# A ring of weight slots: taking a kept slot's entry out of the queue of pools

## The chip, the core and the metric

The kernel runs on one core of a Trainium2 chip. The metric is device time in microseconds (us), taken as the median of several runs. The five engines named below are TensorE (PE; PEld is its weight load), VectorE (DVE), ScalarE (ACT), GpSimd (POOL) and SyncE (SP), whose queue issues nearly all transfers. "DMA" is the core's 16 DMA engines taken together.

## What is computed

One block of a streaming encoder for 256 rows of width 2048: a projection and two kinds of attention, an output projection, and then a mixture of 32 small expert networks, of which each row uses two. Everything the change touches lies in the expert stage and in the norm behind it:

```python
def hierarchical_moe(h, ...):              # t: 256 rows of 2048
    ...                                    # combine: 256 x 32, two non-zero weights per row
    def expert_step(acc, xs):
        wg, wu, wd, c = xs                 # 2048x512, 2048x512, 512x2048
        hid = jax.nn.silu(t @ wg) * (t @ wu)
        return acc + c[:, None] * (hid @ wd), None
...
x = x + hierarchical_moe(rms_norm(x, ffn_norm_gain), ...)
return rms_norm(x, final_norm_gain)
```

## The kernel before

**Stages.** Projection, attention and output projection take about the first 430 us. Then the experts run in 16 pairs, e = 0, 2, ..., 30 (lines 1077 to 1082). For each pair up to 64 rows per expert are gathered into `hT` by matmuls against a selection matrix (`gather`, line 793), so that columns 0 to 63 of an operand belong to the first expert and 64 to 127 to the second. `gates` (line 970) makes 64 matmuls into the bank `pg` with the gate weights and 64 into `pu` with the up weights, `hidden` and `hidden_T` multiply and transpose, `down` (line 1002) makes 64 matmuls into four banks `y` with the down weights, and a pair later `scatter` (line 863) weighs the rows and adds them to the residual rows `x2`. TensorE's instructions are kept in the order of the program (lines 760 to 764).

**Weights and slots.** The weights of a pair, 24 MiB, come in twelve loads of 2 MiB, each into a slot of 128 x 4096 floats. I call them G0 to G3 (gate), U0 to U3 (up) and D0 to D3 (down). G0 holds rows 0 to 1023 of the first expert's gate matrix, G1 those of the second, G2 and G3 rows 1024 to 2047 of the two; U0 to U3 are cut likewise, D0 and D1 are the upper half of the two down matrices, D2 and D3 the lower. In the last pair, e = 30, U2, U3 and D0 to D3 are cut across both experts instead and come in two or four smaller transfers each (lines 887, 1031 and 1045). All loads are issued by SP, which takes its instructions strictly in order: a load that waits for its slot holds up every load behind it.

**The ring.** A slot is a buffer of one of six pools: `ring_a` (4 buffers), `ring_r`, `ring_c` and `ring_d` (2 each), and `ring_h` and `ring_e` (1 each, used only in the first pair). `next_slot` (line 748) hands out slots in a fixed order of pools: the twelve entries of `first` for the first pair, and then, over and over, the ten that are left without h and e:

```python
order = r r c a a a a c d d        # ten entries, ten buffers
```

A pool gives out its oldest buffer that is free; if it has none that is free, the load waits until the last matmul on the load before it in that buffer is done. With ten entries for ten buffers, every load follows the one ten places earlier.

**Two kept slots.** Two requests are not for weights. In the pair e = 28, between gate and up, `z` (line 982) takes a slot and keeps it to the end of the kernel: its left half holds the final norm's gain, spread over all partitions (`gfin`), its right half the first 128 output rows (`fo[0]`). In the last pair, `down_cols` (line 1023) takes another behind its weights for the other 128 output rows (`fo[1]`, line 1048).

**The end.** `down_cols` makes the last products by column cut: 512, 512, 512, 384 and 128 columns wide (j = 0 to 4). `finish(j)` weighs a cut (`yh` on ACT, line 859, and `yl` on DVE, line 860), scatters it by four matmuls, adds it to `x2` (DVE, line 870), and calls `final_block` (line 918), which squares the finished columns on ACT (line 921) with `fo[t]` as the place of the squares and, for the first three cuts, multiplies them by the gain into `fo[t]` (line 924: DVE for t = 0, POOL for t = 1). `final_store` (line 926) adds up the squares, takes the reciprocal root on POOL, scales `fo` and stores it.

Of the kernel before, what the change touches and what calls it, by code (L numbers as in the profile page):

```python
# [24 lines left out]
D = 2048  # L25
# [55 lines left out]
def block_kernel(ctx: ExitStack, tc: tile.TileContext, a: dict, out: bass.AP):  # L81
# [7 lines left out]
    def slot(pl):  # L89
        return pl.tile([P, 4096], F32, tag="slot", name="slot")  # L90
# [221 lines left out]
    def cols_T(accs, name):  # L312
        r = at.tile([P, 4, T], F32, name=name, bufs=2 if name == "q" else 1)
        for b in range(2):
            dve.tensor_tensor(r[:, 2 * b:2 * b + 2], accs[b], bcr(rsb), op=OP.mult)
        return r
# [162 lines left out]
    for g in range(2):  # L479
        c0 = g * 512  # L480
        if g == 0:
# [17 lines left out]
            q, k = cols_T(qa, "q"), cols_T(ka, "k")  # L499
        else:  # L500
            q = cols_T(project_T(c0, False), "q")
# [6 lines left out]
    for g in range(2):  # L508
        c0 = 3072 + g * 512
        q = rope_T(project_T(c0, True), "q")  # L510
# [49 lines left out]
    ring_h = ctx.enter_context(tc.tile_pool(name="ring_h", bufs=1, reuse_waits="tile", side="right"))  # L560
    ring_r = ctx.enter_context(tc.tile_pool(name="ring_r", bufs=NR, reuse_waits="tile", side="right"))
    ring_e = s_e.enter_context(tc.tile_pool(name="ring_e", bufs=1, reuse_waits="tile", side="right"))
# [179 lines left out]
    y_ps = ctx.enter_context(tc.tile_pool(name="y_ps", bufs=4, space=PSUM, reuse_waits="tile"))  # L742

    first = [ring_r, ring_r, ring_c, ring_a, ring_h, ring_a, ring_e, ring_a, ring_a, ring_c, ring_d, ring_d]
    order = [q for q in first if q not in (ring_h, ring_e)]
    units = [0]

    def next_slot():
        units[0] += 1
        u = units[0] - 1  # L750
        return slot(first[u] if u < len(first) else order[(u - len(first)) % len(order)])

    def ps_m():
        return m_ps.tile([P, 512], F32, tag="m", name="m")
# [1 line left out]
    def ps_y():  # L756
        return y_ps.tile([P, 512], F32, tag="y", name="y")


    def mm(*args, **flags):  # L760
        tc.keep_in_program_order(pe.matmul(*args, **flags))  # L761
# [148 lines left out]
    fo = [None, None]  # L910
# [59 lines left out]
    def gates(e, gather_first):  # L970

        last = e == NE - 2
        pg = gu_ps.tile([P, F], F32, name="pg")
        pu = gu_ps.tile([P, F], F32, name="pu")
        for b in range(4):
            if gather_first is not None:
                hT[b] = gather(gather_first, b, 2 if e == 0 else 1)
            gate_up(pg, a["w_gate"], e, b)
        scatter_done((0, 1))
        cT = scatter_mat(sels_of(e))  # L980
        if e == NE - 4:
            z = next_slot()
            gfin[0], fo[0] = z[:, :D], z[:, D:]
            for b in range(NB):
                final_gain(b)
        for b in range(4):
            gate_up(pu, a["w_up"], e, b, last and b > 1)
            if last and b < 2:
                scatter_done((b + 2,))
        if e == 0:  # L990
            keep_rows()
        return cT, hidden(pg, pu, 2 if last else 1)
# [30 lines left out]
    def down_cols(e, cT, hid):  # L1023


        cuts = [(0, 512), (512, 1024), (1024, 1536), (1536, 1920), (1920, D)]
        w = {}
        for h in range(2):
            z = next_slot().rearrange("p (e c n) -> p e c n", e=2, c=2)
            for i in range(2):  # L1030
                sync.dma_start(z[:, i], a["w_down"][e + i, h * 256:h * 256 + 256, :1024]
                               .rearrange("(c p) n -> p c n", p=P))
                for j in range(2):
                    for c in range(2):
                        w[j, i, 2 * h + c] = z[:, i, c, j * 512:j * 512 + 512]
        for j in range(2, 5):
            n0, n1 = cuts[j]
            n = n1 - n0
            if n0 % 512 == 0:
                z = next_slot()  # L1040
                at0 = 0
            for i in range(2):
                zi = z[:, at0:at0 + 4 * n].rearrange("p (c n) -> p c n", c=4)
                at0 += 4 * n
                sync.dma_start(zi, a["w_down"][e + i, :, n0:n1].rearrange("(c p) n -> p c n", p=P))
                for c in range(4):
                    w[j, i, c] = zi[:, c]
        fo[1] = next_slot()[:, :D]
        py = [ps_y() for _ in cuts[:4]]

        def products(j, cs):
            n = cuts[j][1] - cuts[j][0]
            for c in cs:
                for i in range(2):
                    mm(py[j][C * i:C * i + C, :n], hid[:, c, C * i:C * i + C], w[j, i, c],
                       start=c == 0, stop=c == 3)

        def finish(j):
            n0, n1 = cuts[j]

            scatter(cT, weighted(cT, py[j], n1 - n0), n0, n1,
                    lambda t: gu_ps.tile([P, F], F32, name="pu" if j % 2 else "pg") if t else ps_m())
            final_block(n0, n1, j)

        for h in range(2):
            for j in range(2):
                products(j, (2 * h, 2 * h + 1))
        for j in range(2, 5):
            if j == 4:
                py.append(ps_y())  # L1070
            finish(j - 2)
            products(j, range(4))
        finish(3)
        finish(4)
        final_store(len(cuts))
# [106 lines left out]
```

## Time and profile before

| what | value |
|---|---|
| median of 3 runs | 1364.29 us (1363.77 to 1365.88) |
| profiled execution, its own time | 1366.4 us |
| its span on the core | 1364.6 us |
| PE busy | 1308.2 us (96%) |
| DVE, ACT, POOL busy | 491.8, 274.0, 13.6 us |
| TensorE's granted clock, mean | 0.988 |
| DMA, mean over the span | 351 GB/s |

The page cuts the span into 40 equal slices, in which a digit gives a busy share in tenths; the other views list what an engine did in order of time, what it waited for, and what each engine and the DMA did in chosen stretches. A granted clock of 1.00 is 2.4 GHz, one of 0.50 is 1.2 GHz. All times below are microseconds from the start of the profiled span.

### The profile page before, as it was taken

The page shows a single profiled execution, that of the slowest core. Times are in us where ns is not written, and L with a number is a line of the kernel's source. Part 1 is how long each engine was busy: PE and PEld are TensorE (multiplying, and loading weights), DVE is VectorE, ACT ScalarE, POOL GpSimd, SP SyncE. Part 2 cuts the span into 40 slices and gives each one's busy share as a digit, 9 for nine tenths or more (in the row PEclk, how much of TensorE's full clock was granted, in tenths as well). Part 3 has the DMA queues.
Part 4 walks back from the last instruction along what each step waited for, and adds up shares of the span by engine and source line. Part 5 has one row for each costly group of instructions (what it writes and reads, how often), then busy time and mean ns, then how long its engine had stood idle before and what let it go on. Part 6 is the DMA issues. An engine that isn't in the chain of part 4 may idle for free. (4 is left out here: it accounts for less than half of the span.)

```text
span 1364.6 us, 16713 instructions
## 1 busy us (share of the span) xinstructions
PE 1308.2 (96%) x7155; PEld 768.1 (56%) x7155; DVE 491.8 (36%) x906; ACT 274.0 (20%) x454; POOL 13.6 (1%) x22
## 2 busy tenths in 40 slices
PE   9999999999999999999999999999999999999885
PEld 8999998988885444535535444343543434343432
DVE  5555567677643121222322213212221322122123
ACT  6454445354340100000000000000000000001002
POOL 0000000000000000000000000000000000000001
PEclk9999999999999999999999999999999999998988
DMA  9973554446969799999999999999999999999793
GB/s 357 332 261 127 182 186 148 161 166 237 324 232 392 296 428 426 426 427 427 426 427 427 426 426 427 425 427 427 426 428 426 426 428 426 425 427 427 293 407 107
DMA packets 77223, 478.42 MB, mean 351 GB/s; under 512 B 5204, under 2 KB 8148, under 8 KB 53336
## 3 DMA queue, kind: packets, MB, share of 16 engines
q1 hardware_dynamic: 76848, 476.73, 86.0%
q8 instruction: 58, 0.95, 0.3%
q10 hardware_dynamic: 296, 0.56, 0.1%
q14 instruction: 21, 0.17, 0.0%
HBM read 475.18 MB, written 2.10 MB: 350 GB/s over the span
## 5 line engine op out<-in xcount | busy, mean ns | idle before, releaser
L761 PE MATMUL pu<-slot,hT 128*64 128x512 f32 x1024 | 235.2, 601 | 13.5 <-DMA slot<-in_w_up 13.5
L761 PE MATMUL pg<-slot,hT 128*64 128x512 f32 x1024 | 234.3, 598 | 12.3 <-DMA slot<-in_w_gate 12.3
L761 PE MATMUL y<-slot,hid 128*64 128x512 f32 (+2 forms) x1040 | 223.9, 587 | 0.1
L761 PEld LDWEIGHTS pg<-slot,hT 128*64 128x64 f32 x1024 | 75.3, 138 | 165.7 <-issue 153.5
L870 DVE TENSOR_TENSOR x<-x,y 128x512 f32<-128x512 f32 x120 | 75.9, 684 | 252.4 <-PE y L761 252.4
L761 PEld LDWEIGHTS pu<-slot,hT 128*64 128x64 f32 x1024 | 73.9, 138 | 163.7 <-issue 142.8
L761 PEld LDWEIGHTS y<-slot,hid 128*64 128x64 f32 x1040 | 72.8, 137 | 138.5 <-issue 136.0
L257 DVE TENSOR_TENSOR wl<-slot,wh 128x1024 fp32r<-128x1024 f32 (+1 forms) x100 | 117.6, 1181 | 81.5 <-ACT wh L256 81.0
L294 PE MATMUL acc<-xh,wh 128*128 128x256 f32 x512 | 131.5, 289 | 0.0
L294 PE MATMUL acc<-xl,wh 128*128 128x256 f32 x512 | 128.2, 283 | 0.0
L256 ACT ACTIVATE wh<-slot 128x1024 fp32r<-128x1024 f32 (+1 forms) x100 | 101.9, 1025 | 124.5 <-PE acc L279 72.6
L761 PE MATMUL m<-S,slot 128*128 128x128 f32 x960 | 113.7, 277 | 4.7 <-DVE hT L805 4.7
L761 PEld LDWEIGHTS m<-S,slot 128*128 128x128 f32 x960 | 110.5, 192 | 9.7 <-DVE hT L805 7.6
L860 DVE SCALAR_TENSOR_TENSOR yl<-y,ws,yh 128x512 fp32r<-128x512 f32 (+1 forms) x65 | 46.9, 741 | 166.7 <-ACT yh L859 165.1
L294 PEld LDWEIGHTS acc<-xl,wh 128*128 128x128 f32 x512 | 98.0, 191 | 0.4
L294 PEld LDWEIGHTS acc<-xh,wh 128*128 128x128 f32 x512 | 97.9, 191 | 0.5
L859 ACT ACTIVATE yh<-y,ws 128x512 fp32r<-128x512 f32 (+1 forms) x65 | 44.2, 680 | 254.9 <-PE y L761 254.9
L294 PE MATMUL acc<-xh,wl 128*128 128x256 f32 x512 | 82.3, 283 | 0.0
L838 DVE TENSOR_TENSOR sg<-sg,pu 128x512 f32<-128x512 f32 (+1 forms) x17 | 11.1, 655 | 192.6 <-PE pu L761 184.3
L805 DVE TENSOR_TENSOR hT<-m,smallp 128x512 f32<-128x512 f32 (+1 forms) x68 | 44.9, 660 | 91.7 <-PE m L761 91.7
L851 ACT ACTIVATE hid<-m 128x512 f32<-128x512 f32 (+1 forms) x17 | 9.7, 572 | 323.5 <-PE m L764 323.5
L294 PEld LDWEIGHTS acc<-xh,wl 128*128 128x128 f32 x512 | 70.6, 192 | 0.0
(215 smaller groups left out, 1131.8 us busy)
## 6 DMA issues: line engine op xcount, KB each, us to landing
slot<-in_w_down SPq DMA_DIRECT2D x60, 2048.0 KB, 32.6
slot<-in_w_gate SPq DMA_DIRECT2D x60, 2048.0 KB, 36.8
slot<-in_w_up SPq DMA_DIRECT2D x58, 2048.0 KB, 30.6
slot<-in_w_in SPq DMA_DIRECT2D x46, 1024.0 KB, 7.3
slot<-in_w_out SPq DMA_DIRECT2D x16, 1024.0 KB, 5.3
slot<-in_w_up SPq DMA_DIRECT2D x10, 1024.0 KB, 11.6
slot<-in_w_gate SPq DMA_DIRECT2D x8, 1024.0 KB, 9.6
slot<-in_w_down SPq DMA_DIRECT2D x6, 1024.0 KB, 16.1
```

The lines of the kernel that those rows point to most:

```text
L256: act.activation(wh[:, k:k + n], src[:, k:k + n], AF.Copy)
L257: dve.tensor_sub(wl[:, k:k + n], src[:, k:k + n], wh[:, k:k + n].bitcast(F32))
L294: pe.matmul(o, wz[:, i * P:(i + 1) * P], x, start=k == 0 and i % 2 == 0 and wz is wh and x is h, stop=k == KC - 1 and i % 2 == 1 and wz is ...
L761: tc.keep_in_program_order(pe.matmul(*args, **flags))
L805: dve.tensor_tensor(hT[:, j * n:(j + 1) * n], p.rearrange("p (a b) -> p a b", a=n), (gfp if hp_ else gfn)[:, c:c + n, None].to_broadcast([ ...
L838: dve.tensor_tensor(sg[:, q], sg[:, q], pu[:, q], op=OP.mult)
L851: act.activation(hid[:, j * n:(j + 1) * n].rearrange("p c q -> p (c q)"), p[:, :n * P], AF.Copy)
L859: act.activation(yh[:, :n], py[:, :n], AF.Copy, scale=ws)
L860: dve.scalar_tensor_tensor(yl[:, :n], py[:, :n], ws, yh[:, :n].bitcast(F32), op0=OP.mult, op1=OP.subtract)
L870: dve.tensor_tensor(xb, xb, p[:, :n], op=OP.add)
```

## The change

The list of pools becomes a queue. A request takes the entry at its head; the entry goes back to the tail unless it is one of h and e, or the request is marked as kept. The two requests for kept slots are marked.

```diff
     first = [ring_r, ring_r, ring_c, ring_a, ring_h, ring_a, ring_e, ring_a, ring_a, ring_c, ring_d, ring_d]
-    order = [q for q in first if q not in (ring_h, ring_e)]
-    units = [0]
-
-    def next_slot():
-        units[0] += 1
-        u = units[0] - 1
-        return slot(first[u] if u < len(first) else order[(u - len(first)) % len(order)])
+    ring = deque(first)
+
+    def next_slot(keep=False):
+
+        q = ring.popleft()
+        if not keep and q not in (ring_h, ring_e):
+            ring.append(q)
+        return slot(q)
...
         if e == NE - 4:
-            z = next_slot()
+            z = next_slot(keep=True)
             gfin[0], fo[0] = z[:, :D], z[:, D:]
...
-        fo[1] = next_slot()[:, :D]
+        fo[1] = next_slot(keep=True)[:, :D]
```

Up to the request for `z` both kernels ask the same pools in the same order. `z` gets an entry r in both. Behind it stand, before, the same ten entries, two of them r; now nine, one of them r. For the pair e = 28 the eight requests behind `z` still fall on the same pools. From G2 of the last pair on they differ. The table gives, for each load of the last pair, the pool that it asks and the load whose buffer it takes over (28 marks a load of the pair e = 28):

| load | buffer in the listings | before | now |
|---|---|---|---|
| G0 | slot_7663 | d, from G3 (28) | d, from G3 (28) |
| G1 | slot_7665 | r, from U0 (28) | r, from U0 (28) |
| G2 | slot_7683 | r, from G1 | c, from U1 (28) |
| G3 | slot_7685 | c, from U1 (28) | a, from U2 (28) |
| U0 | slot_7735 | a, from U2 (28) | a, from U3 (28) |
| U1 | slot_7737 | a, from U3 (28) | a, from D0 (28) |
| U2 | slot_7775 | a, from D0 (28) | a, from D1 (28) |
| U3 | slot_7786 | a, from D1 (28) | c, from D2 (28) |
| D0 | slot_7810 | c, from D2 (28) | d, from D3 (28) |
| D1 | slot_7813 | d, from D3 (28) | d, from G0 |
| D2 | slot_7816 | d, from G0 | r, from G1 |
| D3 | slot_7819 | r, from G2 | c, from G2 |
| `fo[1]` | slot_7824 | r, from D3 | a, from G3 |

The scheduler, which knows of the waits, orders two queues differently. On SP, the loads of the last pair stood in this order before:

```order
L1014 DMA slot_7643<-in_w_down 128x4096
L895 DMA slot_7663<-in_w_gate 128x4096
L895 DMA slot_7665<-in_w_gate 128x4096
L895 DMA slot_7685<-in_w_gate 128x4096
L895 DMA slot_7735<-in_w_up 128x4096
L895 DMA slot_7683<-in_w_gate 128x4096
L895 DMA slot_7737<-in_w_up 128x4096
L887 DMA slot_7775<-in_w_up 128x2048 x2
```

and now, on the same engine at the same place:

```order
L1015 DMA slot_7643<-in_w_down 128x4096
L896 DMA slot_7663<-in_w_gate 128x4096
L896 DMA slot_7665<-in_w_gate 128x4096
L896 DMA slot_7683<-in_w_gate 128x4096
L896 DMA slot_7685<-in_w_gate 128x4096
L896 DMA slot_7735<-in_w_up 128x4096
L896 DMA slot_7737<-in_w_up 128x4096
L888 DMA slot_7775<-in_w_up 128x2048 x2
```

G2 (slot_7683) has moved from behind G3 and U0 to its place in the program; the line numbers are one higher throughout. On ACT, at the end of the kernel, these stood before (slot_7487 is `fo[0]`, slot_7824 is `fo[1]`, y_7825 to y_7828 and y_7889 are the products of cuts 0 to 4, fss holds the sums of squares):

```order
L859 ACTIVATE yh1_4255<-y_7826,ws_7732 128x512
L921 ACTIVATE slot_7487,fss_4084<-x2_80 128x512
L859 ACTIVATE yh0_4253<-y_7827,ws_7732 128x512
L921 ACTIVATE slot_7487,fss_4084<-x2_80 128x512
L859 ACTIVATE yh1_4255<-y_7828,ws_7732 128x384
L921 ACTIVATE slot_7487,fss_4084<-x2_80 128x512
L921 ACTIVATE slot_7824,fss_4084<-x2_80 128x512 x3
L921 ACTIVATE slot_7487,fss_4084<-x2_80 128x384
L921 ACTIVATE slot_7824,fss_4084<-x2_80 128x384
L859 ACTIVATE yh0_4253<-y_7889,ws_7732 128x128
```

and now:

```order
L860 ACTIVATE yh1_4255<-y_7826,ws_7732 128x512
L922 ACTIVATE slot_7487,fss_4084<-x2_80 128x512
L922 ACTIVATE slot_7824,fss_4084<-x2_80 128x512
L860 ACTIVATE yh0_4253<-y_7827,ws_7732 128x512
L922 ACTIVATE slot_7487,fss_4084<-x2_80 128x512
L922 ACTIVATE slot_7824,fss_4084<-x2_80 128x512
L860 ACTIVATE yh1_4255<-y_7828,ws_7732 128x384
L922 ACTIVATE slot_7487,fss_4084<-x2_80 128x512
L922 ACTIVATE slot_7824,fss_4084<-x2_80 128x512
L860 ACTIVATE yh0_4253<-y_7889,ws_7732 128x128
L922 ACTIVATE slot_7487,fss_4084<-x2_80 128x384
L922 ACTIVATE slot_7824,fss_4084<-x2_80 128x384
```

The squares for `fo[1]` have moved from one block behind the last square of `fo[0]` to their cuts, and the weighing of the last cut (y_7889) to ahead of the 384-wide squares. The order on PE, DVE and POOL is the same in both kernels.

## Rows read from the trace of the kernel before

**Rows 1.** The page's 40 slices of the span (34.1 us each): DMA, busy tenths.

```profile
DMA  9973554446969799999999999999999999999793
```

**Rows 2.** Stretches: us from:to, length, engines' busy us, granted clock, DMA, GB/s.

```profile
core 0: us, PE busy (x) PEld busy (x) DVE busy (x) ACT busy (x) POOL busy (x), PEclk, DMA share, GB/s
1148.00:1207.00 59.00, 56.26 (x282) 24.86 (x280) 13.74 (x27) 3.94 (x6) 0.00 (x0) 1.00 1.01 427
```

**Rows 3.** Waits of PE from 1200 us on: us in total, times, longest.

```profile
PE pg L761 <- DMA slot<-in_w_gate: 8.2, 2, 7.9
```

**Rows 4.** PE in order of time: start us, length us, line, operation, [idle before].

```profile
1243.38 16.92 PE L761 MATMUL pu<-slot,hT 128*64 128x512 f32 x64
...
1270.48 13.95 PE L761 MATMUL y<-slot,hid 128*64 128x512 f32 x64
1284.27 7.04 PE L761 MATMUL pg<-slot,hT 128*64 128x512 f32 x32
1299.18 9.45 PE L761 MATMUL pg<-slot,hT 128*64 128x512 f32 x32 [7.88 <-DMA slot<-in_w_gate]
...
1311.56 3.65 PE L761 MATMUL pu<-slot,hT 128*64 128x512 f32 x16
...
1342.35 2.80 PE L761 MATMUL y<-slot,hid 128*64 128x384 f32 x16
...
1346.21 1.09 PE L761 MATMUL y<-slot,hid 128*64 128x128 f32 x16
...
1350.66 0.33 PE L761 MATMUL m<-yh,cT 128*128 128x128 f32 x1 [2.15 <-ACT yh L859]
```

**Rows 5.** SP's queue in order of time: first issue, time to the last one's end.

```profile
1234.21 20.05 SPq L895 DMA_DIRECT2D slot<-in_w_gate  x3
1260.32 0.33 SPq L895 DMA_DIRECT2D slot<-in_w_up  x1
1291.34 0.33 SPq L895 DMA_DIRECT2D slot<-in_w_gate  x1
```

**Rows 6.** Stretches in the last pair, columns as in the group on stretches above.

```profile
1279.00:1285.10 6.10, 6.10 (x30) 2.01 (x28) 1.50 (x2) 1.37 (x2) 0.00 (x0) 1.00 0.56 236
1285.10:1291.70 6.60, 6.20 (x30) 1.87 (x26) 0.00 (x0) 0.00 (x0) 0.00 (x0) 1.00 0.00 0
1291.70:1335.50 43.80, 35.31 (x146) 12.71 (x148) 7.88 (x14) 3.32 (x6) 0.00 (x0) 0.88 1.00 384
1299.10:1303.50 4.40, 4.32 (x11) 1.40 (x13) 0.00 (x0) 0.00 (x0) 0.00 (x0) 0.50 0.96 408
1305.00:1308.50 3.50, 3.50 (x18) 1.07 (x14) 0.00 (x0) 0.00 (x0) 0.00 (x0) 1.00 1.00 418
```

**Rows 7.** Loads issued by line 895 from 1180 us on: time to landing.

```profile
DMA to landing us min/median/max: 7.7/24.9/39.2
```

**Rows 8.** ACT in order of time at the end.

```profile
1347.40 0.64 ACT L921 ACTIVATE slot<-x 128x512 f32<-128x512 f32 x1
...
1349.76 0.51 ACT L921 ACTIVATE slot<-x 128x384 f32<-128x384 f32 x1
...
1350.27 0.35 ACT L859 ACTIVATE yh<-y,ws 128x128 fp32r<-128x128 f32 x1
```

**Rows 9.** DVE in order of time at the end.

```profile
1345.85 0.69 DVE L870 TENSOR_TENSOR x<-x,m 128x512 f32<-128x512 f32 x1 [1.31 <-PE m L761]
...
1347.58 0.68 DVE L924 TENSOR_TENSOR slot<-x,slot 128x512 f32<-128x512 f32 x1
...
1348.67 0.55 DVE L870 TENSOR_TENSOR x<-x,pu 128x384 f32<-128x384 f32 x1
1350.65 0.35 DVE L860 SCALAR_TENSOR_TENSOR yl<-y,ws,yh 128x128 fp32r<-128x128 f32 x1 [1.43 <-ACT yh L859]
...
1352.47 0.16 DVE L927 TENSOR_REDUCE frs<-fss 128x2 f32<-128x10 f32 x1 [0.54 <-ACT slot L921]
```

**Rows 10.** POOL in order of time at the end.

```profile
1348.20 3.73 POOL L924 TENSOR_TENSOR slot<-x,slot 128x512 f32<-128x512 f32 x3 [939.48 <-ACT slot L921]
```

## What I expected, before the changed kernel ran

> **What bounds the kernel now.** I read the 40 slices first, then the stretches, then PE's waits and PE, SP, ACT and DVE in order of time around each hole. In the slices the DMA is at 9 from the fourteenth on, save one digit 7 near 1262 to 1296 us and the tail [rows 1]. One steady pair shows why: 59 us hold 56.26 us of PE work at the full clock, and the DMA at 427 GB/s [rows 2]; twelve loads of 2.097 MB at that rate are 58.9 us, so 4.91 us for one. Loads bound the expert stage, and PE follows a few per cent behind. The hole in the DMA is therefore worth a look. From 1285.1 to 1291.7 it moved nothing, and from 1279.0 to 1285.1 it ran at 236 GB/s, its queues running dry one after another [rows 6]; those 6.1 us hold 1.44 MB, 3.4 us of full rate, so it ran dry at about 1282.4 in the mean. In SP's queue nothing was issued between 1260.3 and 1291.34, and then it was a gate load [rows 5]: G2, whose slot is r from G1. Pool r had one buffer left, the other being the kept one, so G2 had to wait until PE had used up G1, which it did at 1284.27 + 7.04 = 1291.31 [rows 4]. G2 landed 7.7 us after its issue, the shortest time in its view [rows 7], and PE stood still for it from the end of its first 32 gate products: 7.88 us before 1299.18 [rows 4], nearly all that PE waits for gate loads from 1200 us on [rows 3].
>
> **Part 1: the stall at G2, removed.** G2 now takes c from U1 (28), and stands in SP's queue where G3 stood, third of the gate loads, the last of which was issued by 1234.21 + 20.05 = 1254.3 [rows 5]. The 7.88 us go if G2 and G3 land by 1291.3. G3 and U0 now wait for U2 and U3 of pair 28, used up at the end of that pair's up products, 1243.38 + 16.92 = 1260.3 [rows 4]; that is when U0 was issued before [rows 5]. So G3 takes the place that U0 had in the stream of bytes, landed at 1285.1 at the latest [rows 6]: 6 us to spare.
>
> Something else goes with the stall. The 32 gate products behind it took 9.45 us, the 32 ahead of it 7.04 [rows 4]. The granted clock was 1.00 before the stall, 0.50 (1.2 GHz) from 1299.1 to 1303.5 behind 7.88 us in which PE did nothing, and 1.00 again from 1305 [rows 6]. Without the idle time I see no reason for the lower clock: 9.45 - 7.04 = 2.41 us more. The bounds of this term are 0 and 2.41; I take 2.41, since the 64 down products just ahead ran at the full clock with the same kind of work. Sum of part 1: 7.88 + 2.41 = 10.29 us.
>
> **What is late next.** Every later load has a new holder to wait for, and SP is in order. U1 and U2 now wait for D0 and D1 (28), used up at half the down products, 1270.48 + 13.95/2 = 1277.5 [rows 4]; behind them in SP's queue stand U3 and the D loads. Before, U1's buffer was free at 1260.3, but U1 was queued behind G2 and left only at 1291.7. At 1277.5 the DMA has U0 still to bring: with one load more in its stream it runs dry at 1282.4 + 4.91 = 1287.3 in the mean, so there is no hole. U3 and D0 wait for D2 and D3 (28), done at 1284.4, D1 and D2 for G0 and G1, done at 1291.3, D3 for G2, done 7.04 us later: each is issued before the loads ahead of it are through. The eight last loads took 43.8 us at 384 GB/s from 1291.7 [rows 6]; now they follow without a hole, so they end between 1282.4 + 43.8 = 1326.2 and 1285.1 + 43.8 = 1328.9. PE's needs, all moved up by 10.3: the first up product at 1301.3 (U0 and U1 land by 1285.1 + 2 x 4.91 = 1294.9), the first product of D3 at 1342.35 - 10.3 = 1332.1 [rows 4]. The smallest margin is 3.2 us, with both doubts taken against me. I cost the new waits at nothing; the backlog of 10 us that stands in the DMA at 1277.5 hides them, and if it weren't there each microsecond of lateness beyond the margin would be one of PE.
>
> **Part 2: the tail.** Before, `fo[1]` took over r from D3, so nothing could be written there before the last products ended at 1346.21 + 1.09 = 1347.30 [rows 4]. At 1347.40 ACT began a block of squares that ran to 1349.76 + 0.51 = 1350.27, and only then came the weighing of the last cut [rows 8], though its products were there at 1347.30. DVE idled 1.43 us for it and PE 2.15 [rows 9, 4]. Now `fo[1]` is an a buffer from G3, long free, and each square follows its cut. The weighing comes behind one square for `fo[1]`, which can start at 1347.40 as a like one did [rows 8], so it begins near 1348.05 in old times, 2.2 us earlier. But then DVE is what is late: it is busy through 1348.67 + 0.55 = 1349.22 [rows 9], and `yl` starts there instead of at 1350.65. The gain is the 1.43 us of DVE's idle time, and what hangs behind (four short products, two adds, two squares, the sum at 1352.47) moves as a block. The 384-wide squares now run beside `yl` and end by 1349.9, ahead of the last cut's. From the sum on all is the same work. Bounds: 0 (another engine late) and 2.2 (DVE not late); I take 1.43, the row that waits there.
>
> POOL's three multiplies move too. Before, they ran in a block of 3.73 us, 1.24 each, from 1348.20 [rows 10], just as DVE's own last one ended (1347.58 + 0.68 [rows 9]); now each follows its cut. Whether one beside a multiply of DVE slows it, this trace doesn't show: DVE's 384-wide add beside POOL took 0.55 us, where a 512-wide one without POOL had taken 0.69 [rows 9]. In the last cut DVE's multiply would start at 1347.58 and POOL's not before ACT's square for it ends, some 1348.05, so I cost it at nothing; if POOL were first and DVE had to wait it out, the 1.43 would shrink by up to 1.24. On this the Trainium skill has a rule that speaks against the change ("SBUF — State Buffer", section "Who interferes with whom"): a VectorE instruction with two SBUF inputs and a GpSimd instruction that reads SBUF exclude each other, and the second waits for the whole of the first. By that rule and the order of starts above it is POOL that waits, some 0.2 us, and the sum stays; with the order reversed the tail would gain 0.2 us instead of 1.4.
>
> **The sum.** 10.29 + 1.43 = 11.7 us. The profiled execution's span would go from 1364.6 to 1352.9, its own time from 1366.4 to 1354.7. The three runs' median, 1364.29, lies 2.1 us below the profiled time; the stall is one of order and not of chance, so I take the same 11.7 us off: 1352.6 us.
>
> **Rivals.** (a) The tail gives nothing: POOL and DVE get in each other's way, or another engine's work fills the 1.43 us. Then 1364.3 - 10.3 = 1354.0. For it: DVE has hardly a gap from 1345.85 to 1349.22 [rows 9]. Against: the two multiplies start apart, as above. 10%. (b) The stall moves on: a load lands late and PE waits some 3 to 4 us for it, as where my margin of 3.2 us for D3 is used up twice over. 1352.6 + 3.5 = 1356.1. For it: the stage is bound by loads, and the last ones are small pieces at 384 instead of 427 GB/s [rows 6]. Against: the hole of 9 us that closes is larger than what any load lacks. 7%. (c) The clock stays low for as long as behind the stall: 1355.0. 2%. (d) Slower: issue to landing is a fixed time and no backlog. U1 is issued at 1277.5 at the earliest and needed at 1301.3. If it took the 39.2 us that the slowest of its line took [rows 7], it would land at 1316.7, PE would stand for 15.4 us in another place and lose the clock's 2.4 as well: 1352.6 + 17.8 = 1370.4. It decides from 24 us on, and costs more than the change gains from 33. Against: with an empty queue the same load took 7.7 us [rows 7], so the 39.2 are time in the queue; by my count U1 finds 10 us ahead of it. 3%. (e) The edit does nothing that counts, 1364.3: the listings show G2's move, so 1%.
>
> **How the numbers follow.** The forecast has 77%: 1352.6, by itself 1351 to 1354. The range goes from 1350.6 (the tail's upper bound and 1.2 us for how far medians differ) to 1356.5, which takes in (a), (c) and most of (b). A measurement of this kernel can tell about 0.2%, 2.7 us, from no change. All cases but (d) and (e) are faster by more: 0.95; within 0.2%: 0.02; slower: 0.03.
>
> **What would show it.** Part 1: SP issues third and fourth gate loads of the last pair by 1254 and near 1260, the DMA has no empty stretch there, and the 64 gate products run as one group of about 14.1 us at clock 1.00; PE's wait for gate loads falls to under 1 us. A wait of PE for an up or down load in the last pair would show (b) or (d), and a clock under 1 in the gate products (c). Part 2: the weighing of the last cut on ACT right behind one square, no idle time ahead of `yl`, and the sum 5.2 - 1.4 = 3.7 us behind the end of the last products instead of 5.2. The forecast is wrong if PE's last products end less than 9 us earlier.

## The result, and the profile after

The changed kernel took 1351.21 us in the median of four runs (1350.44 to 1354.62); the kernel before, measured with it, 1364.03 us (1363.13 to 1365.88, four runs). The ratio is 0.9911, with an interval of 0.9898 to 0.9924: about 12.1 us less (10.4 to 13.9). The profiled execution's own time is 1351.83 us, its span 1350.1 us. Line numbers are one higher than before.

The slices of the page, to be held against [rows 1]; the digit 7 at 1262 to 1296 us has gone, and every digit from the fifteenth to the last but one is now 9:

```profile
DMA  9973554546869799999999999999999999999993
```

SP's queue in order of time (first issue, time to the last one's end), against [rows 5]:

```profile
1233.77 24.74 SPq L896 DMA_DIRECT2D slot<-in_w_gate  x4
1258.61 17.18 SPq L896 DMA_DIRECT2D slot<-in_w_up  x2
1275.88 9.92 SPq L888 DMA_DIRECT2D slot<-in_w_up  x6
```

All four gate loads stand in one row and are out by 1258.5; U0 follows at once, and U1 at 1275.5, when half of the down products of e = 28 are done. The 31 us in which SP issued nothing are gone; what is left are two pauses of some 17 us, before 1251.3 and before 1275.5, in which the DMA goes on at 427 to 428 GB/s. The same two stretches as in [rows 6], and two more to the end of the loads (columns: stretch, length, busy us of PE, PEld, DVE, ACT and POOL, granted clock, DMA share, GB/s):

```profile
1279.00:1285.10 6.10, 6.10 (x30) 2.01 (x28) 1.50 (x2) 1.38 (x2) 0.00 (x0) 1.00 1.00 424
1285.10:1291.70 6.60, 6.60 (x34) 2.28 (x32) 0.00 (x0) 0.00 (x0) 0.00 (x0) 1.00 1.00 422
1291.70:1326.00 34.30, 33.29 (x150) 12.05 (x148) 9.94 (x18) 4.71 (x9) 0.00 (x0) 1.00 0.95 363
1326.00:1330.00 4.00, 4.00 (x20) 1.55 (x18) 1.83 (x3) 1.44 (x5) 1.54 (x1) 1.00 0.03 8
```

Where the DMA had moved 236 GB/s and then nothing it now moves 424 and 422, and the clock is 1.00 throughout. But for some 0.03 MB the weights are in by about 1326. PE in order of time (start, length, line, operation, idle time before it in brackets), against [rows 4]:

```profile
1242.08 16.07 PE L762 MATMUL pu<-slot,hT 128*64 128x512 f32 x64
...
1268.35 13.95 PE L762 MATMUL y<-slot,hid 128*64 128x512 f32 x64
1282.13 13.90 PE L762 MATMUL pg<-slot,hT 128*64 128x512 f32 x64
...
1298.95 3.65 PE L762 MATMUL pu<-slot,hT 128*64 128x512 f32 x16
...
1329.76 2.80 PE L762 MATMUL y<-slot,hid 128*64 128x384 f32 x16
...
1333.62 1.09 PE L762 MATMUL y<-slot,hid 128*64 128x128 f32 x16
...
1336.94 0.33 PE L762 MATMUL m<-yl,cT 128*128 128x128 f32 x1 [0.96 <-DVE yl L861]
```

The 64 gate products of the last pair are one row without idle time, 13.90 us from start to end where the two rows before had taken 24.30 (1284.27 to 1308.63). The end of the kernel on ACT, DVE and POOL, each against its rows before [rows 8, 9, 10]:

```profile
1334.62 0.61 ACT L922 ACTIVATE slot<-x 128x512 f32<-128x512 f32 x1
...
1335.23 0.35 ACT L860 ACTIVATE yh<-y,ws 128x128 fp32r<-128x128 f32 x1
```

```profile
1334.99 0.68 DVE L925 TENSOR_TENSOR slot<-x,slot 128x512 f32<-128x512 f32 x1
...
1336.08 0.55 DVE L871 TENSOR_TENSOR x<-x,pu 128x384 f32<-128x384 f32 x1
1336.55 0.34 DVE L861 SCALAR_TENSOR_TENSOR yl<-y,ws,yh 128x128 fp32r<-128x128 f32 x1
...
1338.36 0.16 DVE L928 TENSOR_REDUCE frs<-fss 128x2 f32<-128x10 f32 x1 [0.54 <-ACT slot L922]
```

```profile
1326.83 1.54 POOL L925 TENSOR_TENSOR slot<-x,slot 128x512 f32<-128x512 f32 x1 [919.07 <-ACT slot L922]
1331.54 1.54 POOL L925 TENSOR_TENSOR slot<-x,slot 128x512 f32<-128x512 f32 x1 [3.17 <-ACT slot L922]
1335.40 1.41 POOL L925 TENSOR_TENSOR slot<-x,slot 128x512 f32<-128x512 f32 x1 [2.32 <-ACT slot L922]
```

The weighing of the last cut stands right behind one square, DVE goes from its 384-wide add into `yl` without a pause, and POOL's multiplies are spread over the cuts.

**Where the time went.** The two profiled spans differ by 14.5 us. Cut at the same events:

| stretch | before | after | less by |
|---|---|---|---|
| to the start of the gate products of e = 30 | 1284.27 | 1282.13 | 2.14 |
| gate products, with the start of what follows them | 27.29 | 16.82 | 10.47 |
| from there (first up product) to the end of the last products | 35.74 | 35.76 | 0.0 |
| to the sum of squares on DVE | 5.17 | 3.65 | 1.52 |
| to the end | 12.1 | 11.7 | 0.4 |

The first row is not the change's: the first load that takes another buffer, G2, is not used before the row below. Of its 2.14 us, 0.45 are there before the gain's matmuls of the pair e = 28 begin, and 1.70 come in these and the up products behind them, where it differs from execution to execution how far the clock falls (last experiment). The last row, where the arithmetic is the same, I don't count either. What is left, 10.5 + 1.5 = 12.0 us, agrees with the 12.1 of the ratio.

### The profile page after: what moved, and what is told of

Same layout as the page of the kernel before. It is cut to its first block, busy times and chain, and to the rows that moved or that the text cites. A ratio compares the mean times of both kernels' runs of the same rounds, so it can differ in the third digit from the quotient of the medians.

```text
span 1350.1 us, 16715 instructions
## 1 busy us (share of the span) xinstructions
PE 1303.3 (97%) x7155; PEld 769.0 (57%) x7155; DVE 491.6 (36%) x906; ACT 274.1 (20%) x454; POOL 14.4 (1%) x22
## 4 chain that ended last, share of the span: by engine, by line
PE 72%; DMA 23%; DVE 3%; ACT 0%; issue 0%; SPq 0%; POOLq 0%; DVEq 0%; POOL 0%
DMA slot<-in_w_up 20%; PE y L762 14%; PE acc L294 14%; PE pu L762 12%; PE m L762 9%; PE pg L762 8%; PE acc L277 4%; PE acc L278 4%; PE acc L279 4%; DMA slot<-in_w_gate 3%; DVE hT L806 1%; DVE x L871 1%; PE lg L593 1%; PE ps L411 0%; DMA slot<-in_w_in 0%
## 5 line engine op out<-in xcount | busy, mean ns | idle before, releaser
L762 PE MATMUL pg<-slot,hT 128*64 128x512 f32 x1024 | 230.6, 593 | 3.9 <-DMA slot<-in_w_gate 3.9
L257 DVE TENSOR_TENSOR wl<-slot,wh 128x1024 fp32r<-128x1024 f32 (+1 forms) x100 | 117.5, 1180 | 80.6 <-ACT wh L256 80.3
```

Source lines behind the costliest of these rows:

```text
L257: dve.tensor_sub(wl[:, k:k + n], src[:, k:k + n], wh[:, k:k + n].bitcast(F32))
```

## Experiments

Theory: two separate gains, about 10.4 us from G2's place in the ring (7.9 of waiting, 2.4 of clock) and 1.5 us from `fo[1]`'s buffer. Rivals: the one gain needs the other; the clock would have been low anyway; the order of POOL and DVE is indifferent; fewer ring entries cost something that the change hides.

### One part without the other

The changed kernel with the tail's buffers as before (D2 in c, D3 in r, `fo[1]` in r behind D3; the diff is against the changed kernel):

```diff
-                z = next_slot()
+                z = slot(ring_c if j == 2 else ring_r)
...
-        fo[1] = next_slot(keep=True)[:, :D]
+        fo[1] = slot(ring_r)[:, :D]
```

> The changed kernel, but D2 asks pool c and D3 pool r, and the slot for the second half of the output rows (fo[1]) asks r, so that it takes over D3's buffer as before the change. Theory (two separate gains, 10.3 us at the gate load G2 and 1.4 us in the tail): the 64 gate products of the last pair stay one group of 13.9 us without a wait, the block of squares behind the last products is back, idle time of 1.4 us ahead of the last yl on DVE is back, and the sum of the squares stands 5.2 us behind the end of the last products instead of 3.65; the time is 1.5 us above the changed kernel's, some 1352.7. Rival (the tail's gain comes of the loads being earlier, not of fo[1]'s buffer): the sum stays 3.65 us behind and the time at 1351.2.

The kernel before with only `fo[1]` moved to an a buffer:

```diff
-        fo[1] = next_slot()[:, :D]
+        fo[1] = slot(ring_a)[:, :D]
```

> The kernel before, with fo[1] alone moved to a buffer of pool a that is long free. Theory: the stall of 7.9 us at G2 and the slow gate products behind it (9.45 us for 32) stay, the sum of squares comes 3.65 us behind the last products instead of 5.2: 1364.0 - 1.5 = 1362.5. Rival (the two gains are not independent, the tail's needs the earlier loads): no gain, 1364.

The first took 1353.22 us (1353.04 to 1355.32, four runs), the second 1362.58 (1359.79 to 1364.72, ten), the kernel before beside them 1363.46 (13 runs): ratios 0.9924 (0.9904 to 0.9945) and 0.9993 (0.9981 to 1.0004). By time the first keeps most of the gain, and the second can't be told from no change; 1.5 us is too little for that. The traces say it more sharply. PE and DVE in order of time in the first:

```profile
1281.96 13.90 PE L762 MATMUL pg<-slot,hT 128*64 128x512 f32 x64
...
1333.45 1.09 PE L762 MATMUL y<-slot,hid 128*64 128x128 f32 x16
...
1337.89 0.35 DVE L861 SCALAR_TENSOR_TENSOR yl<-y,ws,yh 128x128 fp32r<-128x128 f32 x1 [1.43 <-ACT yh L860]
1339.70 0.16 DVE L928 TENSOR_REDUCE frs<-fss 128x2 f32<-128x10 f32 x1 [0.47 <-ACT slot L922]
```

and in the second:

```profile
1299.34 8.93 PE L761 MATMUL pg<-slot,hT 128*64 128x512 f32 x32 [8.31 <-DMA slot<-in_w_gate]
...
1345.84 1.09 PE L761 MATMUL y<-slot,hid 128*64 128x128 f32 x16
...
1350.58 0.16 DVE L927 TENSOR_REDUCE frs<-fss 128x2 f32<-128x10 f32 x1 [0.54 <-ACT slot L921]
```

In the first there is no stall, but DVE's idle 1.43 us are back to the hundredth, and the sum comes 1339.70 - 1334.54 = 5.16 us behind the last products. In the second the stall is there (8.31) and the sum comes 1350.58 - 1346.93 = 3.65 us behind them, as in the changed kernel. The two gains are separate and add up.

### Was the clock the stall's doing?

The kernel before, with products added whose result nothing reads, in the place where PE stands still. First 34 of them, all into the same half of the columns:

```diff
+            if last and b == 2:
+                p = ps_m()
+                for _ in range(34):
+                    mm(p[:C], hT[0][:, 0, :C], part[0, 0], start=True, stop=True)
             gate_up(pg, a["w_gate"], e, b)
```

> The kernel before, with 34 more matmuls (64 x 512, into a spare bank that nobody reads, on operands that are there) between the first and the second 32 gate products of the last pair, so that PE works through most of its wait for G2. Theory (the granted clock fell because PE stood idle): the clock stays at 1.00, the 32 products behind the wait take 7.0 us instead of 9.45, G2 still lands at the same time, and the whole is 2.4 us faster: 1361.6. Rival (the clock falls for another reason, or the 9.45 us are a matter of operands just landing): the 32 products stay at 9.4 us and the time at 1364.

It took 1384.01 us (ratio 1.0148, 1.0127 to 1.0168), far off the expectation, because the filler was mis-sized. PE in order of time:

```profile
1289.22 28.92 PE L761 MATMUL m<-slot,hT 128*64 128x512 f32 x67
1318.03 7.40 PE L761 MATMUL pg<-slot,hT 128*64 128x512 f32 x31
```

Two things made the filler four times too long. Each matmul of the program shows as two records in these listings, so that 34 make 68, of which 67 stand in the row (the counts of 32 and 64 that the text gives for gate, up and down products are counts of records too). And 28.92 us for 67 records are 0.43 us each, at a granted clock of 1.00, twice the 0.22 of the gate products, which go into the two halves by turns. The question has a first answer all the same: the gate products behind the filler took 7.40 us, not 9.45. The second try has 16 matmuls, 32 records, alternating between the halves:

```diff
+            if last and b == 2:
+                p = ps_m()
+                for n in range(16):
+                    i = n % 2
+                    mm(p[C * i:C * i + C], hT[0][:, 0, C * i:C * i + C], part[0, 0], start=True, stop=True)
             gate_up(pg, a["w_gate"], e, b)
```

> The kernel before, with 16 more matmuls of the same kind as the gate products (into a spare bank that nobody reads, on operands that are there, alternating between the two halves of the columns, so about 7.0 us in all) between the first and the second half of the gate products of the last pair: PE works through most of its wait for G2. The 34 of the run before took 28.9 us, since all lay in one half of the columns; there the products behind them took under 7.9 us at clock 1.00, but the added work hid the size. Theory (the clock fell because PE stood idle): G2 lands at the same time, PE waits under 1 us, the second half of the gate products takes 7.0 us instead of 9.45, and the whole is 2.4 us faster than before. Rival (it is the operands just landing that make them slow): 9.4 us, and no gain.

PE in order of time, and the stretch of the last row (columns as above):

```profile
1280.43 7.04 PE L761 MATMUL pg<-slot,hT 128*64 128x512 f32 x32
1287.30 7.04 PE L761 MATMUL m<-slot,hT 128*64 128x512 f32 x32
1295.44 7.09 PE L761 MATMUL pg<-slot,hT 128*64 128x512 f32 x32 [1.10 <-DMA slot<-in_w_gate]
1295.44:1302.50 7.06, 7.06 (x33) 2.25 (x33) 0.00 (x0) 0.00 (x0) 0.00 (x0) 1.00 0.99 421
```

G2 is as late as before and PE still stands for 1.10 us, but the clock is 1.00 and the second half of the gate products takes 7.09 us instead of 9.45. From the end of the first half to the end of the second it is 15.06 us, against 17.32 in the kernel before [rows 4]: 2.26 us gained by work that is thrown away. The median is lower too, 1362.02 against 1363.44 us, but the ratio, 0.9992 (0.9981 to 1.0003), can't tell as little from no change; the trace carries this. So the term of 2.41 us was the price of standing still, and the low clock needs no cause of its own.

### POOL and DVE at the gain

The changed kernel with the two multiplies of a cut exchanged: the one for `fo[0]`, whose square is ready first, on POOL, the other on DVE.

```diff
-                (pool if t else dve).tensor_tensor(...)
+                (dve if t else pool).tensor_tensor(...)
```

> The changed kernel with the two multiplies by the final gain exchanged: POOL takes the rows t = 0, whose squares come first, DVE the rows t = 1. POOL's multiply then starts about 0.3 us before DVE's instead of after it. Theory of the prediction's sum (they do not hinder each other): DVE's stays at 0.68 us and starts 0.3 us later, POOL's takes 1.24; the time rises by at most 0.3 us. Rival (they exclude each other, the first one holds the second up): DVE's multiply is held up, ends up to 1.2 us later than POOL starts plus its own time, the sum of squares comes up to 0.9 us later than in the changed kernel (4.5 us behind the last products), and POOL's takes 1.24 us, less than the 1.41 to 1.54 that it took in the changed kernel.

It took 1353.02 us (1352.3 to 1353.32, four runs; ratio 0.9916, 0.9897 to 0.9935). The line's instructions (engine, operation, count; shortest, median and longest in ns; first and last start in us), and then the engines in order of time at the last cut:

```profile
L925 POOL TENSOR_TENSOR slot<-x,slot x3: 1274/1277/1281, 1326.7 to 1335.3; 128x512 f32<-128x512 f32 x3
L925 DVE TENSOR_TENSOR slot<-x,slot x3: 1253/1256/1258, 1327.3 to 1335.8; 128x512 f32<-128x512 f32 x3
```

```profile
1334.10 1.09 PE L762 MATMUL y<-slot,hid 128*64 128x128 f32 x16
1335.27 1.28 POOL L925 TENSOR_TENSOR slot<-x,slot 128x512 f32<-128x512 f32 x1 [2.59 <-ACT slot L922]
1335.84 1.26 DVE L925 TENSOR_TENSOR slot<-x,slot 128x512 f32<-128x512 f32 x1 [0.28 <-ACT slot L922]
1340.04 0.16 DVE L928 TENSOR_REDUCE frs<-fss 128x2 f32<-128x10 f32 x1 [0.47 <-ACT slot L922]
```

All three of DVE's multiplies took about 1.25 us, against 0.68 in the changed kernel, and POOL's now take 1.27 to 1.28, nearly the 1.24 of the block without DVE [rows 10], against 1.41 to 1.54. So whichever starts second is the one held. The sum comes 1340.04 - 1335.19 = 4.85 us behind the last products instead of 3.65: the exchange costs 1.2 us, four fifths of the tail's gain. Not all of it is the holding: DVE's multiply is 0.58 us longer, it also starts 0.37 us later behind the last products, because the exchange gives DVE the square that is ready second, and the remaining 0.25 us come in the short steps behind it.

### Fewer entries in the ring

If a fixed time from issue to landing were what counts, as in rival (d), a shorter ring should hurt. The changed kernel with `fo[1]` taken at e = 28, which leaves eight entries for the last pair:

```diff
             gfin[0], fo[0] = z[:, :D], z[:, D:]
+            fo[1] = next_slot(keep=True)[:, :D]
...
-        fo[1] = next_slot(keep=True)[:, :D]
```

> The changed kernel with the slot for fo[1] taken and kept already in the pair e = 28, so that the ring has eight entries from there on instead of nine; every load of the last two pairs then waits for one load later. Theory (what covers the new waits is the backlog of the DMA, 10 us where U1 is issued): the loads are issued later, up to 15 us for G0 and G1, but the DMA has 26 us of work queued there, it never runs dry, and PE waits for nothing new: within 1 us of the changed kernel, 1351.2 to 1352. Rival (the time from issue to landing is fixed, so each entry less costs the run-ahead of one load): PE waits for loads, 5 us or more: 1356 or above.

and with three kept slots, which leaves seven:

```diff
-            z = next_slot(keep=True)
-            gfin[0], fo[0] = z[:, :D], z[:, D:]
+            gfin[0], fo[0], fo[1] = (next_slot(keep=True)[:, :D] for _ in range(3))
...
-        fo[1] = next_slot(keep=True)[:, :D]
```

> The changed kernel with three slots kept in the pair e = 28 (the gain and the two halves of the output rows apart), so that the ring has seven entries from there on. Theory (backlog): G3 and U0 are now issued at 1275, U1 and U2 at 1282, U3 and D0 at 1289, where the DMA has its queue nearly empty (it would run dry near 1275); here the cover ends: the DMA shows a first hole of 0 to 2 us, the loads for the up products land within 4 us of their need, and the time is 0 to 3 us above the changed kernel's. Rival (fixed landing time): 10 us or more above it.

Eight entries took 1352.2 us (1351.41 to 1354.33), seven 1354.12 (1350.73 to 1354.21); ratios 0.9919 (0.9899 to 0.994) and 0.9922 (0.99 to 0.9944) to the kernel before at 1363.44. SP's queue with seven entries, a stretch of the DMA, and the gate products:

```profile
1253.73 7.73 SPq L896 DMA_DIRECT2D slot<-in_w_gate  x4
1277.45 7.18 SPq L896 DMA_DIRECT2D slot<-in_w_up  x2
```

```profile
1280.00:1285.00 5.00, 5.00 (x26) 1.61 (x24) 1.50 (x2) 1.38 (x2) 0.00 (x0) 1.00 0.96 406
```

```profile
1284.11 13.90 PE L762 MATMUL pg<-slot,hT 128*64 128x512 f32 x64
```

The first gate load leaves 20 us later than in the changed kernel and the first up load 19 us later, the other gate and up loads of these rows 3 to 9 us, and nothing comes of it: no hole in the DMA (I had expected one of up to 2 us), and PE waits for no load in the last pair. From issue to landing the gate and up loads from 1180 us on took, in the changed kernel (line 896) and with seven entries (the same line):

```profile
DMA to landing us min/median/max: 19.8/27.6/39.6
DMA to landing us min/median/max: 11.7/18.7/39.2
```

A load that leaves later lands sooner after its issue. The slower median with seven entries is not the ring's as far as its profile goes: there the gate products start 1.98 us later than in the changed kernel, and the stretch in front of them that varies by itself (below) is 1.7 us longer, while from their start to the sum of squares it is 56.22 us, and 56.23 in the changed kernel. So it was not the number of free buffers that the kernel before suffered from. It suffered from asking a pool with one free buffer twice in a row, with everything else queued behind the second request.

### What the ends are bound by now

The changed kernel with the gain brought by one broadcast transfer of 1 MiB in place of four matmuls and four ACT copies; and the same with that slot asked for between D2 and D3, so that the ring keeps ten entries until then:

```diff
...
-        p = ps_m()
-        mm(p, ident[:NB, b:b + 1].to_broadcast([NB, P]), rows_[2], start=True, stop=True)
-        act.activation(gfin[0][:, b * 512:(b + 1) * 512], p, AF.Copy)
+        if b == 0:
+            act.dma_start(gfin[0], a["final_gain"].to_broadcast([P, D]))
...
```

```diff
...
+        if b == 0:
+            sync.dma_start(gfin[0], a["final_gain"].to_broadcast([P, D]))
...
+            if n0 == 1536:
+                z = next_slot(keep=True)
+                gfin[0], fo[0] = z[:, :D], z[:, D:]
+                final_gain(0)
             if n0 % 512 == 0:
                 z = next_slot()
...
```

> The changed kernel with the final gain spread over the partitions by one transfer of 1 MiB from ACT's queue in the pair e = 28, in place of four matmuls and four evictions. PE saves 5.5 us of matmuls there and the low clock behind them, 2.2 us more; the DMA gets 2.5 us more to bring. Theory (the loads now bound the end: at the run with 128-row matmuls PE had begun to wait for D2): PE's 7.7 us can't be had; PE waits for loads in the last two pairs, the last load lands 2.5 us later, and the time is 1350 to 1352. Rival (PE still bounds the last pairs): 1351.5 - 7.7 = 1344.

> As the run before, but the slot for gain and output rows is taken in the last pair, between the loads D2 and D3, and the gain's transfer is issued there: no slot is kept in the pair e = 28, and the ring has its ten entries to the end. Theory (what counts is the bytes ahead of D3, not the number of entries): the same as the run before within 1 us, 1350 to 1352, with PE's wait for loads at D3 and, on DVE, for the gain. Rival (the tenth entry is worth a load's run-ahead, up to 4.9 us): 1345 to 1347.

1351.21 us (1350.79 to 1352.0) and 1351.65 (1351.42 to 1353.01), beside 1352.14 (1350.2 to 1353.42) for the changed kernel on the same chip: at most 1 us better. PE saves the gain's matmuls, and waits for loads in their place. PE's longest waits for loads in the two kernels from 1180 us on (total, times, longest), the first two rows from the first, the others from the second:

```profile
PE pu L762 <- DMA slot<-in_w_up: 3.7, 2, 2.0
PE pg L762 <- DMA slot<-in_w_gate: 3.0, 2, 2.7
```

```profile
PE pu L762 <- DMA slot<-in_w_up: 3.4, 2, 1.7
PE y L762 <- DMA slot<-in_w_down: 1.8, 2, 1.2
```

In the changed kernel PE waits 2.4 us for loads in that stretch (1.7 for an up load and 0.7 for a gate load), in the first of these two 6.7: the extra MiB, 2.5 us of the DMA at 427 GB/s, stands ahead of the weights. With the transfer put late and ten entries kept until then, the wait moves to the down loads, and the clock falls behind it (PE's last products but one):

```profile
1329.26 4.48 PE L762 MATMUL y<-slot,hid 128*64 128x384 f32 x14 [1.23 <-DMA slot<-in_w_down]
```

Fourteen of these sixteen records take 4.48 us at a granted clock of 0.62, where all sixteen took 2.80 in the changed kernel. PE's saving is given back either way, in waits for loads and in what follows them. That speaks for the bytes as what bounds the end once the hole is closed; a run that takes bytes away was not made.

### Where the run-to-run spread comes from

The four executions of the changed kernel lie 4 us apart. The place shows in the granted clock during and behind the four matmuls that spread the gain (`m<-g,c`, from 1236.7 us on), where the up products of e = 28 run. Stretches of the changed kernel:

```profile
1237.00:1242.00 5.00, 4.66 (x8) 1.27 (x6) 3.18 (x9) 1.80 (x4) 0.00 (x0) 0.76 1.00 426
1242.00:1252.00 10.00, 10.00 (x39) 3.08 (x40) 0.00 (x0) 0.60 (x1) 0.00 (x0) 0.78 1.00 424
```

PE is busy for 4.66 of the first 5 us and all of the next 10, and yet the clock is 0.76 and 0.78. The gain's matmuls have operands of four rows. The same sums with the operands padded with zeros to 128 rows:

```diff
-                      acts.tile([NB, 512], F32, name="g4")))
-        act.dma_start(rows_[2], a["final_gain"])
+                      acts.tile([P, 512], F32, name="g4")))
+        pool.memset(rows_[2], 0.0)
+        act.dma_start(rows_[2][:NB], a["final_gain"])
...
-        mm(p, ident[:NB, b:b + 1].to_broadcast([NB, P]), rows_[2], start=True, stop=True)
+        mm(p, ident[:, b:b + 1].to_broadcast([P, P]), rows_[2], start=True, stop=True)
```

> The changed kernel, with the final gain's four matmuls in the pair e = 28 made 128 rows deep instead of 4 (a tile whose other 124 rows are zero, and a one-hot row of 128 instead of one of 4). Seen in all profiles so far: the granted clock falls to 0.5 in and behind the 4-row matmuls, which take 5 to 6.6 us with what follows them, and the 64 up products behind them 15.4 to 16.9 us instead of 13.9. Theory (few rows at work let the clock fall, as idling did at G2): the clock stays at 1.00, the four matmuls take 3.4 us, the up products 13.9, together some 4 us less; the loads of the last pair have a margin of 3.7 us, so 1347.2, or up to 0.5 us more. Rival (the fall has another cause): no change from 1351.2.

```profile
1237.00:1242.00 5.00, 4.13 (x13) 1.37 (x13) 3.70 (x10) 2.74 (x5) 0.00 (x0) 1.00 1.01 429
1242.00:1256.00 14.00, 14.00 (x65) 4.62 (x66) 0.09 (x1) 0.18 (x1) 0.00 (x0) 1.00 1.00 425
```

The clock stays at 1.00, with PE idle a little longer than before (busy for 4.13 of the first 5 us). The time was 1349.8 us (1349.55 to 1350.05, five runs), ratio 0.9898 (0.9881 to 0.9914) to the kernel before, and not the 1347.2 that I had expected. Once more, beside the changed kernel on one chip:

> The changed kernel itself, beside the others of this group on one chip. All theories: 1351 to 1352, with executions that spread over some 4 us (1350.4 to 1354.6 so far), as in the kernel before (1361.5 to 1366.4), since the fall of the clock behind the 4-row matmuls comes at a different moment each time.

> The version with the final gain's matmuls 128 rows deep, on the same chip as the changed kernel. It took 1349.8 with executions within 0.5 us. Theory (the clock's fall at the 4-row matmuls sets the spread, and the loads bound what is left): again within 1 us of each other and 1.4 to 2 us faster than the changed kernel. Rival (it was the chip or the hour): the same median and the same spread as the changed kernel.

The changed kernel took 1352.14 us (1350.2 to 1353.42, four runs) and the padded one 1349.66 (1348.88 to 1349.97, four runs); to the kernel before at 1365.71 the ratios are 0.9906 (0.9889 to 0.9922) and 0.9884 (0.9867 to 0.99). The padded kernel is 2.5 us below the changed one on the same chip, and its nine runs, which lie within 1.2 us, are all below the changed kernel's eight: the fastest version found. From the first of these matmuls to the end of the up products it is 18.7 and 18.8 us in its two profiles; in the kernels with four rows it was 20.1 to 23.2 (ten profiles: 23.2 in the kernel before, 21.5 and 20.2 in the two of the changed one; both ends of the range are found, within 0.2 us, with either order of the loads). I had counted on some 17.3 us, 3.4 of them for the four matmuls; these took 3.9, and the stretch holds two short waits besides, 0.5 us for DVE and 0.3 for an up load. A little less reached the end than the stretch gave. The third group of its last down products:

```profile
1322.72 4.02 PE L762 MATMUL y<-slot,hid 128*64 128x512 f32 x16
```

That is 4.02 us where the changed kernel's take 3.65, and the weight loads among them wait 0.18 us for a down load. That PE now catches up with the loads is my reading of it; the other profile of this kernel has 3.98 us there and shows no such wait.

## Why the prediction was right, step by step

**The forecast** of 1352.6 us lies 1.4 above the median of 1351.21 and within the spread of the runs; the second set of the changed kernel gave 1352.14. The sum of 11.7 us compares with 12.0 in the trace and 12.1 by the ratio.

Two slips in the working change nothing: the DMA's digits are at 9 from the fifteenth slice on, not the fourteenth, and the chances of the cases that are faster add up to 0.96, where I gave 0.95.

**The stall and the clock**, predicted at 7.88 + 2.41 = 10.29, came out at 10.47. SP's third and fourth gate loads left by 1252.1 and 1258.5 (predicted: 1254 and near 1260), the stretch without bytes is gone, and the gate products are one group of 13.90 us at clock 1.00 (I had said 14.1). That the clock's share belongs to the stall was an argument from the order of events ("I see no reason for the lower clock"); the filler of 16 matmuls shows it. Rival (c) falls with the clock of 1.00 behind the place of the stall.

**The new waits**, costed at nothing, cost nothing: from the first up product to the end of the last products both kernels take the same 35.7 us, and the last pair has no wait of PE for a load. The loads ended at about 1326, where I had put them between 1326.2 and 1328.9, and D3's first product came at 1329.76, a margin of some 3.7 us (at least 3.2 predicted). Rival (b) falls. So does rival (d): U1 left at 1275.5, near the 1277.5 that I had put, and PE did not wait for it, and with seven entries it left at 1284.3 and still landed in time. The time to landing [rows 7] was in the main time in the queue, as the forecast argued from its shortest value: with seven entries its median fell from 27.6 to 18.7 us.

**The tail**, predicted at 1.43, gave 1.52. What was to be late next was named rightly: PE idles 0.96 us, and it is DVE's `yl` that it waits for, and DVE's pause of 1.43 us is gone. Rival (a) falls by the two kernels with one part each.

**POOL and DVE.** I had put the order of starts so that POOL would be the one to wait, 0.2 us at no price. It did: 1.41 us in the last cut where the block before had 1.24 each, while DVE's stayed at 0.68. The Trainium skill's rule ("SBUF — State Buffer", section "Who interferes with whom"), by which the two exclude each other, holds here. For the other order I had put a price of up to 1.24 us, and the exchanged kernel's tail is 1.2 us longer; but only 0.58 us of this is DVE's longer multiply, so the agreement is in part luck. In that order DVE's multiply ended 0.55 us behind the end of POOL's (1337.10 and 1336.55), a little less than the 0.68 it takes by itself, so the wait is nearly, not quite, for the whole of the first.

**The part left out.** I took the span up to the last pair for the same in both kernels. It isn't the same from one execution to the next: the clock in and behind the gain's matmuls moves it by up to 3 us, more than the whole tail is worth. In the two profiles this came to 1.7 us in favour of the change, with 0.45 us more ahead of these matmuls, and a reader of the two spans alone would have counted 14.5. The forecast wasn't hurt, because the sum was made of terms and set against the median.

**What the diff's second mark does.** The request for `fo[1]` is the last of the kernel, so taking its entry out of the ring can change nothing; all of the gain, the tail's too, comes from the one entry that `z` takes with it, which shifts every later request.

## What to carry to other kernels

A hole in a stage that is bound by transfers is worth more than its length suggests: ask which single request the in-order queue stood behind, and whose buffer that request was waiting for. The number of buffers mattered little here (with nine, eight or seven entries PE waited for no load in the last pair); a request for a buffer that can't come free in time, with everything queued behind it, cost 10 us. When two changes act at once, cut both traces at common events and leave out what differs ahead of the first changed instruction.

## What the runs showed of the hardware that I had not expected

- TensorE's clock fell while TensorE was busy: to 0.76 and 0.78 in the mean during and behind matmuls of four rows, 0.68 and 0.65 in the same place in the kernel before, and 1.00 with 128 rows of mostly zeros. With 128 rows the kernel is 2.5 us shorter, and its nine runs lie within 1.2 us, where the changed kernel's eight lie within 4.4.
- Products thrown away can pay: 7 us of filler in a wait of 7.9 us left the products behind it 2.26 us earlier in the end.
- Matmuls of 64 columns that all go into one half of the columns took 0.43 us a record, by turns into both halves 0.22, both at a clock of 1.00. The first also all used the same weights; no run takes the two apart.
- POOL's multiply of 128 x 512 took 1.24 us each in the block without DVE, 1.41 to 1.54 when DVE's had started ahead of it; DVE's took 0.68 ahead and 1.25 behind.
